# Delta-rule blocks in a fixed order, with the decay prepared a head ahead

## The chip, the cores and the metric

One core of a Trainium2 chip runs one program. The metric is the device time of one execution in microseconds; the figure for a kernel is the median of several. The core has TensorE (PE, with its weight loader PEld), VectorE (DVE), ScalarE (ACT), GpSimd (POOL), and SyncE (SP), which here issues the DMAs.

## The reference

A hybrid decoder layer on x of 2048 x 1024, all float32: a norm, one input projection of 9224 columns, two token mixers side by side, and an output projection. The part that matters here is the first mixer, gated DeltaNet with 4 heads of 128 channels, in chunks of 64 tokens:

```python
qkv = silu(causal_depthwise_conv(dn_qkv, conv_w))      # 4 taps
q = l2_normalize(q) * 128 ** -0.5;  k = l2_normalize(k)
gc = cumsum(g)                                         # per chunk, per head
decay = exp(where(causal, gc[i] - gc[j], -inf))
lower = where(strict, (beta * k) @ k.T * decay, 0)
a_intra = where(causal, q @ k.T * decay, 0)
# then (I + lower)^-1, u, w, and a scan over the chunks
```

The second mixer is a dilated sliding-window attention; its part of the kernel is not changed.

## The kernel before

The program runs in stages: attention with its projections; three projection units for gates (`z_block`), beside which the last attention tiles drain; the delta-rule stage; the remaining gate units, beside which VectorE inverts the chunk matrices and the scan runs; and the output.

In the delta-rule stage `cunits` goes through twelve units, for each head h one of keys, one of queries, one of values (`k_block`, `q_block`, `v_block`). A unit has 4 blocks of 512 tokens. A block is 24 matmuls of 128x512 into a PSUM tile `mm` (three buffers): float32 is split in a high and a low part, three products for each of 8 slices. After every second slice `self.hook()` runs, so a hook is six wide matmuls and a block four hooks. `self.at(d, f)` runs `f` d hooks later. It is the way in which small TensorE work of a block (transposes, key-key and query-key products) is put between the wide matmuls of later blocks. `fn(n, pr)` is the block's function, called when its 24 matmuls are issued.

`conv` copies the block to `xr` (ScalarE), multiplies by the last tap into `acc` (ScalarE), adds three taps (VectorE, L629), takes a tanh (ScalarE) and multiplies (VectorE, L632), all at once in the program. `k_block` then loads the cumulated decay of the block, broadcast over 128 partitions, into `gcb` (512 KB, one buffer), adds the causal mask (VectorE, L650), takes four differences (L654) and four exponentials into `E` (ScalarE, L656). At hooks 8 and 9 it transposes the keys in pairs (L663) and ScalarE empties the two PSUM tiles `tp`, with a sum of squares (L667) and a scaling (L668). `q_block` splits keys and queries into a high part `kqh` (ScalarE) and a low part `kql` (L699 on GpSimd for keys, L701 on VectorE for queries), whole blocks with one buffer; at hooks 8 and 9 it transposes queries (L709) and multiplies (L710 to L712) into `sc`, and VectorE multiplies by `E` into `la` (L715), which five DMAs store. `v_block` transposes and scales.

What sets the order: in this stage nothing is fixed by hand. The framework's scheduler orders each engine's instructions by its own estimate of times and by buffers. In the attention stage `pinned` fixes the order of PE, ACT, DVE and POOL as written; SP's, after the first loads, is the scheduler's.

Of the kernel before, what the change touches and what calls it, by code (L numbers as in the profile page):

```python
# [6 lines left out]
F32 = mybir.dt.float32  # L7
# [5 lines left out]
P = 128  # L13
# [3 lines left out]
NB = 4  # L17
# [23 lines left out]
class Net:  # L41
# [574 lines left out]
    def conv(self, n, ct, pr, dst):  # L616
        nc, dp = self.nc, self.dp
        xr = dp.tile([P, 515], F32, name="xr", bufs=2)
        if n == 0:
            nc.gpsimd.memset(xr[:, 0:3], 0.0)  # L620
        else:
            nc.vector.tensor_copy(xr[:, 0:3], self.xr[:, 512:515])
        self.xr = xr
        nc.scalar.activation(xr[:, 3:515], pr, AF.Copy)
        acc = dp.tile([P, 512], F32, name="acc", bufs=2)
        w = self.cw[:, ct, :]
        nc.scalar.activation(acc, pr, AF.Identity, scale=w[:, 3:4])  # L627
        for j in (2, 1, 0):
            nc.vector.scalar_tensor_tensor(out=acc, in0=xr[:, j:j + 512], scalar=w[:, j:j + 1], in1=acc,  # L629
                                           op0=ALU.mult, op1=ALU.add)  # L630
        nc.scalar.activation(dst, acc, AF.Tanh, scale=0.5)
        nc.vector.scalar_tensor_tensor(out=dst, in0=dst, scalar=1.0, in1=acc, op0=ALU.add, op1=ALU.mult)  # L632
# [4 lines left out]

    def k_block(self, h, n, pr):
        nc, dp = self.nc, self.dp
        if n == 0:  # L640
            self.kT = dp.tile([P, T], F32, name="kT", bufs=1)
            self.E = dp.tile([P, 16, P], F32, name="E", bufs=1)
        kT, E = self.kT[:, n * 512:(n + 1) * 512], self.E
        self.conv(n, 4 + h, pr, kT)
        self.recput(n, h, R_KT, P, kT.rearrange("p (a c) -> p a c", c=P))
        gcb = dp.tile([P, 2, 4, P], F32, name="gcb", bufs=1)
        nc.sync.dma_start(gcb.rearrange("p a b c -> p a (b c)"),
                          dr(self.gcscr, h * T + n * 512, [[0, P], [H * T, 2], [1, 512]]))
        En = E[:, n * 4:n * 4 + 4, :]
        nc.vector.tensor_tensor(out=gcb[:, 1], in0=gcb[:, 1], in1=self.cmask.unsqueeze(1).to_broadcast([P, 4, P]),  # L650
                                op=ALU.add)
        for t in range(4):
            c = h * 16 + n * 4 + t
            nc.vector.scalar_tensor_tensor(out=gcb[:, 0, t], in0=gcb[:, 0, t], scalar=self.ngc[:, c:c + 1],  # L654
                                           in1=gcb[:, 1, t], op0=ALU.add, op1=ALU.add)
            nc.scalar.activation(En[:, t, :], gcb[:, 0, t], AF.Exp, bias=self.nlc[:, c:c + 1])  # L656
        ss = dp.tile([P, 12], F32, name="ss", bufs=2)
        kd = dp.tile([P, 4, P], F32, name="st4", bufs=2)

        def pe(t0):  # L660
            pt = self.ps.tile([P, 512], F32, name="tp", bufs=2)
            for t in (t0, t0 + 1):
                nc.tensor.transpose(pt[:, (t - t0) * P:(t - t0 + 1) * P], kT[:, t * P:(t + 1) * P], self.ident)  # L663
            for t in (t0, t0 + 1):
                c = h * 16 + n * 4 + t
                a = pt[:, (t - t0) * P:(t - t0 + 1) * P]
                nc.scalar.activation(kd[:, t, :], a, AF.Square, accum_out=ss[:, t:t + 1])  # L667
                nc.scalar.activation(kd[:, t, :], a, AF.Identity, scale=self.ek[:, c:c + 1])  # L668
            if t0 == 2:
                fin()  # L670

        def fin():
            cs = slice(h * 16 + n * 4, h * 16 + n * 4 + 4)
            self.recput(n, h, R_KD, P, kd)
            G = nc.gpsimd
            G.tensor_scalar(out=ss[:, 0:4], in0=ss[:, 0:4], scalar1=4 * EPS, scalar2=None, op0=ALU.add)
            G.tensor_tensor(out=ss[:, 4:8], in0=ss[:, 0:4], in1=self.mhalf[:, 0:4], op=ALU.pow)
            G.tensor_tensor(out=ss[:, 8:12], in0=ss[:, 4:8], in1=self.beta[:, cs], op=ALU.mult)
            G.tensor_scalar(out=self.vss[:, cs], in0=ss[:, 8:12], scalar1=0.5, scalar2=None, op0=ALU.mult)
            G.tensor_tensor(out=ss[:, 8:12], in0=ss[:, 8:12], in1=ss[:, 4:8], op=ALU.mult)  # L680
            G.tensor_scalar(out=self.nbr[:, cs], in0=ss[:, 8:12], scalar1=-1.0, scalar2=None, op0=ALU.mult)
            G.tensor_tensor(out=self.ksn[:, cs], in0=self.nbr[:, cs], in1=self.egc[:, cs], op=ALU.mult)
        self.at(8, lambda: pe(0))
        self.at(9, lambda: pe(2))

    def q_block(self, h, n, pr):
        nc, dp = self.nc, self.dp
        qT = dp.tile([P, 512], F32, name="qT", bufs=2)
        self.conv(n, h, pr, qT)
        self.recput(n, h, R_QT, P, qT.rearrange("p (a c) -> p a c", c=P))  # L690
        kT, E = self.kT, self.E
        ss = dp.tile([P, 12], F32, name="ss", bufs=2)
        sq = dp.tile([P, P], F32, name="sq", bufs=1)
        kqh = dp.tile([P, 4, 2, P], F32R, name="kqh", bufs=1)
        kql = dp.tile([P, 4, 2, P], F32R, name="kql", bufs=1)
        la = dp.tile([P, 4, 2, P], F32, name="la", bufs=1)
        kv, qv = (a.rearrange("p (a c) -> p a c", c=P) for a in (kT[:, n * 512:(n + 1) * 512], qT))
        nc.scalar.activation(kqh[:, :, 0, :], kv, AF.Copy)
        nc.gpsimd.tensor_tensor(out=kql[:, :, 0, :], in0=kv, in1=kqh[:, :, 0, :].bitcast(F32), op=ALU.subtract)  # L699
        nc.scalar.activation(kqh[:, :, 1, :], qv, AF.Copy)  # L700
        nc.vector.tensor_tensor(out=kql[:, :, 1, :], in0=qv, in1=kqh[:, :, 1, :].bitcast(F32), op=ALU.subtract)  # L701

        def pe(t0):
            pt = self.ps.tile([P, 512], F32, name="tp", bufs=2)
            pk = self.ps.tile([P, 512], F32, name="sc", bufs=2)
            for t in (t0, t0 + 1):
                b = pk[:, (t - t0) * 256:(t - t0) * 256 + 256]
                rh, rl = (a[:, t].rearrange("p a c -> p (a c)") for a in (kqh, kql))
                nc.tensor.transpose(pt[:, (t - t0) * P:(t - t0 + 1) * P], qT[:, t * P:(t + 1) * P], self.ident)  # L709
                nc.tensor.matmul(b, kqh[:, t, 0, :], rh, start=True, stop=False)  # L710
                nc.tensor.matmul(b, kqh[:, t, 0, :], rl, start=False, stop=False)
                nc.tensor.matmul(b, kql[:, t, 0, :], rh, start=False, stop=True)  # L712
            for t in (t0, t0 + 1):
                nc.scalar.activation(sq, pt[:, (t - t0) * P:(t - t0 + 1) * P], AF.Square, accum_out=ss[:, t:t + 1])
            nc.vector.tensor_tensor(out=la[:, t0:t0 + 2], in0=pk.rearrange("p (a b c) -> p a b c", b=2, c=P),  # L715
                                    in1=E[:, n * 4 + t0:n * 4 + t0 + 2, :].unsqueeze(2).to_broadcast([P, 2, 2, P]),
                                    op=ALU.mult)
            if t0 == 2:
                cs = slice(h * 16 + n * 4, h * 16 + n * 4 + 4)
# [6 lines left out]
                G = nc.gpsimd  # L726
                G.tensor_scalar(out=ss[:, 0:4], in0=ss[:, 0:4], scalar1=4 * EPS, scalar2=None, op0=ALU.add)
                G.tensor_tensor(out=ss[:, 4:8], in0=ss[:, 0:4], in1=self.mhalf[:, 0:4], op=ALU.pow)
                G.tensor_scalar(out=self.cq[:, cs], in0=ss[:, 4:8], scalar1=SCALE, scalar2=None, op0=ALU.mult)
        self.at(8, lambda: pe(0))  # L730
        self.at(9, lambda: pe(2))

    def v_block(self, h, n, pr):
        nc, dp = self.nc, self.dp
        vT = dp.tile([P, 512], F32, name="qT", bufs=2)
        self.conv(n, 8 + h, pr, vT)
# [10 lines left out]
        self.at(8, pe)  # L747
# [284 lines left out]
    def run(self):  # L1032
# [27 lines left out]

        def open_dn():
# [3 lines left out]
            self.dp = pool(dst, "dp", "right")  # L1065

        def start_inverse():
            self.nb_out()
            dst.close()
# [103 lines left out]
```

## Time and profile before

| | |
|---|---|
| device time, median of 3 | 2399.8 us (2398.44 to 2401.62) |
| profiled execution | 2395.87 us, span 2394.1 us |
| granted TensorE clock, mean | 0.995 |
| TensorE busy | 2350.5 us, 98% |
| delta-rule stage | about 1118 to 1430 us of the span |

Times in the views count from the start of the span. An idle time stands before the instruction that ended it, with what released it. Busy TensorE time is the union of its matmuls, whose ends are modelled: wide ones show some 0.39 us each but start closer together.

### The profile page before, as it was taken

The page shows a single profiled execution, that of the slowest core. Times are in us where ns is not written, and L with a number is a line of the kernel's source. Part 1 is how long each engine was busy: PE and PEld are TensorE (multiplying, and loading weights), DVE is VectorE, ACT ScalarE, POOL GpSimd, SP SyncE. Part 2 cuts the span into 40 slices and gives each one's busy share as a digit, 9 for nine tenths or more (in the row PEclk, how much of TensorE's full clock was granted, in tenths as well). Part 3 has the DMA queues.
Part 4 walks back from the last instruction along what each step waited for, and adds up shares of the span by engine and source line. Part 5 has one row for each costly group of instructions (what it writes and reads, how often), then busy time and mean ns, then how long its engine had stood idle before and what let it go on. Part 6 is the DMA issues. An engine that isn't in the chain of part 4 may idle for free.

```text
span 2394.1 us, 40632 instructions
## 1 busy us (share of the span) xinstructions
PE 2350.5 (98%) x13640; PEld 2136.8 (89%) x13640; DVE 1169.7 (49%) x2819; ACT 856.6 (36%) x3021; POOL 824.0 (34%) x1803
## 2 busy tenths in 40 slices
PE   8999999999999999999999999999999999999999
PEld 7899999999999999988777878888888878889988
DVE  5543344334434434344666666999344433454431
ACT  6433333444434444334665662111233313111110
POOL 6633333333333334301442451101233212433441
PEclk9999999999999999999999999999999999999999
DMA  8443344333333335233454443222567645555442
GB/s 283 156 115 111 107 122 120 104 101 108 109 97 111 111 91 128 85 94 103 126 128 117 117 106 118 68 75 75 191 203 207 184 150 158 155 175 161 147 141 75
DMA packets 378808, 307.30 MB, mean 128 GB/s; under 512 B 61352, under 2 KB 345320, under 8 KB 378216
## 3 DMA queue, kind: packets, MB, share of 16 engines
q1 hardware_dynamic: 378312, 304.64, 43.5%
q8 instruction: 108, 1.77, 0.3%
q14 instruction: 100, 0.82, 0.1%
q10 hardware_dynamic: 288, 0.07, 0.0%
HBM read 187.92 MB, written 116.69 MB: 127 GB/s over the span
## 4 chain that ended last, share of the span: by engine, by line
PE 86%; DMA 4%; DVE 3%; POOL 3%; ACT 2%; issue 2%; SPq 0%; ACTq 0%; DVEq 0%; POOLq 0%
PE mm L238 10%; PE mm L240 10%; PE mm L239 10%; PE mm L524 9%; PE mm L526 9%; PE mm L525 9%; PE mm L1014 2%; PE mm L1016 2%; PE mm L1015 2%; PE mm L997 2%; PE mm L999 2%; PE mm L998 2%; DMA gcb<-gcscr 2%; PE po L333 2%; PE tp L290 2%
## 5 line engine op out<-in xcount | busy, mean ns | idle before, releaser
L238 PE MATMUL mm<-wh,hh 128*128 128x384 f32 (+1 forms) x1536 | 554.4, 361 | 6.1 <-ACT hh L131 2.7
L240 PE MATMUL mm<-wh,hl 128*128 128x384 f32 (+1 forms) x1536 | 519.3, 338 | 2.7 <-DVE hl L135 2.7
L239 PE MATMUL mm<-wl,hh 128*128 128x384 f32 (+1 forms) x1536 | 517.8, 337 | 0.7 <-DVE wl L79 0.6
L524 PE MATMUL mm<-hh,wh 128*128 128x512 f32 x1152 | 464.8, 403 | 0.0
L526 PE MATMUL mm<-hh,wl 128*128 128x512 f32 x1152 | 454.5, 395 | 0.0
L525 PE MATMUL mm<-hl,wh 128*128 128x512 f32 x1152 | 453.1, 393 | 0.0
L238 PEld LDWEIGHTS mm<-wh,hh 128*128 128x128 f32 x1536 | 289.6, 189 | 10.5 <-ACT wh L78 4.3
L240 PEld LDWEIGHTS mm<-wh,hl 128*128 128x128 f32 x1536 | 288.9, 188 | 4.1 <-DVE hl L135 4.1
L239 PEld LDWEIGHTS mm<-wl,hh 128*128 128x128 f32 x1536 | 290.5, 189 | 1.7 <-DVE wl L79 1.1
L526 PEld LDWEIGHTS mm<-hh,wl 128*128 128x128 f32 x1152 | 217.3, 189 | 47.3
L524 PEld LDWEIGHTS mm<-hh,wh 128*128 128x128 f32 x1152 | 217.6, 189 | 43.0
L525 PEld LDWEIGHTS mm<-hl,wh 128*128 128x128 f32 x1152 | 217.8, 189 | 41.2
L263 DVE SCALAR_TENSOR_TENSOR rec<-mm,st,wqk 128x128 f32<-128x128 f32 x384 | 116.7, 346 | 264.4 <-POOL st L255 239.4
L79 POOL TENSOR_TENSOR wl<-raw,wh 128x512 fp32r<-128x512 f32 (+1 forms) x73 | 104.2, 1439 | 409.4 <-ACT wh L78 409.2
L317 ACT ACTIVATE p<-sc,ol 128x128 f32<-128x128 f32 (+1 forms) x192 | 82.0, 427 | 315.8 <-DVE ol L315 273.3
L253 POOL TENSOR_SCALAR st<-st 128x2 f32<-128x2 f32 x192 | 37.7, 196 | 400.9 <-ACT rec L249 399.5
L249 ACT ACTIVATE rec<-mm 128x128 f32<-128x128 f32 x384 | 102.4, 272 | 185.3 <-PE mm L240 171.3
L997 PE MATMUL mm<-oh,hh 128*128 128x256 f32 x512 | 143.8, 281 | 3.1 <-DVE gt L1001 2.9
L999 PE MATMUL mm<-oh,hl 128*128 128x256 f32 x512 | 142.9, 279 | 0.0
L998 PE MATMUL mm<-ol,hh 128*128 128x256 f32 x512 | 142.9, 279 | 0.0
L629 DVE SCALAR_TENSOR_TENSOR acc<-xr,cw,acc 128x512 f32<-128x512 f32 x144 | 121.7, 845 | 41.9 <-ACT acc L627 37.7
L255 POOL TENSOR_TENSOR st<-st,mhalf 128x2 f32<-128x2 f32 x192 | 134.7, 702 | 16.0
(243 smaller groups left out, 4283.8 us busy)
## 6 DMA issues: line engine op xcount, KB each, us to landing
rscr<-rec SPq DMA_DIRECT2D x192, 192.0 KB, 1.9
raw<-in_w_in_dram SPq DMA_DIRECT2D x138, 256.0 KB, 3.0
qk<-rscr SPq DMA_DIRECT2D x192, 128.0 KB, 2.2
gscr<-gt SPq DMA_DIRECT2D x64, 256.0 KB, 2.4
gt<-gscr SPq DMA_DIRECT2D x64, 256.0 KB, 3.4
oscr<-ol SPq DMA_DIRECT2D x192, 65.0 KB, 2.0
oc<-oscr SPq DMA_DIRECT2D x16, 780.0 KB, 5.2
v<-rscr SPq DMA_DIRECT2D x192, 64.0 KB, 2.0
```

What stands on the lines that cost most here:

```text
L238: nc.tensor.matmul(pr[:, :w], a, wh[:, k, :w], start=(k == 0), stop=False)
L239: nc.tensor.matmul(pr[:, :w], a, wl[:, k, :w], start=False, stop=False)
L240: nc.tensor.matmul(pr[:, :w], b, wh[:, k, :w], start=False, stop=(k == KT - 1))
L255: nc.gpsimd.tensor_tensor(out=st[:, 2:4], in0=st[:, 0:2], in1=self.mhalf[:, 0:2], op=ALU.pow)
L263: nc.vector.scalar_tensor_tensor(out=qk[:, j, :], in0=pr[:, j * P:(j + 1) * P], scalar=st[:, 2 + j:3 + j], in1=s["w"][2][:, j, :], op0=ALU ...
L524: nc.tensor.matmul(pr, wh[:, k, :], a, start=(k == 0), stop=False)
L525: nc.tensor.matmul(pr, wh[:, k, :], b, start=False, stop=False)
L526: nc.tensor.matmul(pr, wl[:, k, :], a, start=False, stop=(k == KT - 1))
L629: nc.vector.scalar_tensor_tensor(out=acc, in0=xr[:, j:j + 512], scalar=w[:, j:j + 1], in1=acc, op0=ALU.mult, op1=ALU.add)
L997: nc.tensor.matmul(o, self.wbh[:, k, ms], oh[:, k, :], start=(k == b * 4), stop=False)
L998: nc.tensor.matmul(o, self.wbh[:, k, ms], ol[:, k, :], start=False, stop=False)
L999: nc.tensor.matmul(o, self.wbl[:, k, ms], oh[:, k, :], start=False, stop=(k == b * 4 + 3))
```

## The change

- The order of PE, ACT, DVE and POOL is fixed as written (`pinned(False)`: SP's is not) from `open_dn`, ahead of the first key unit, to `start_inverse`.
- The decay is a chain of its own, `e_chain`: load at its start, mask 4 hooks later (now on GpSimd), differences after 5 (VectorE, straight into `E`), exponentials after 7, in place. Head 0's blocks start 7 hooks apart at the stage's beginning; head h + 1's start with the first value block of head h, 5 hooks apart. `E` has four buffers of one block; `gcb` still has one.
- In `conv` tanh and the last multiply (`gate`) come 4 hooks later, right ahead of the next block's convolution. For keys and queries the first tap moves to VectorE; the clearing of `xr` too.
- Key transposes at hooks 7 and 9, their sums at 11; values at 7.
- `kqh` and `kql` are made in pairs of 128 tokens, two buffers, both low parts on GpSimd, at hooks 6 and 7; query products at 9 and 10, with both transposes ahead of the six products; the sums at 12.

```diff
-    def conv(self, n, ct, pr, dst):
+    def conv(self, n, ct, pr, dst, then):
...
-            nc.gpsimd.memset(xr[:, 0:3], 0.0)
+            nc.vector.memset(xr[:, 0:3], 0.0)
...
-        nc.scalar.activation(acc, pr, AF.Identity, scale=w[:, 3:4])
+        if ct < 8:
+            nc.vector.tensor_scalar(out=acc, in0=pr, scalar1=w[:, 3:4], scalar2=None, op0=ALU.mult)
+        else:
+            nc.scalar.activation(acc, pr, AF.Identity, scale=w[:, 3:4])
...
-        nc.scalar.activation(dst, acc, AF.Tanh, scale=0.5)
-        nc.vector.scalar_tensor_tensor(out=dst, in0=dst, scalar=1.0, in1=acc, op0=ALU.add, op1=ALU.mult)
+        def gate():
+            nc.scalar.activation(dst, acc, AF.Tanh, scale=0.5)
+            nc.vector.scalar_tensor_tensor(out=dst, in0=dst, scalar=1.0, in1=acc, op0=ALU.add, op1=ALU.mult)
+            then()
+        self.at(4, gate)
...
+    def e_chain(self, h, period, n=0):
+        if h == H:
+            return
+        nc, dp = self.nc, self.dp
+        gcb = dp.tile([P, 2, 4, P], F32, name="gcb", bufs=1)
+        nc.sync.dma_start(gcb.rearrange("p a b c -> p a (b c)"),
+                          dr(self.gcscr, h * T + n * 512, [[0, P], [H * T, 2], [1, 512]]))
+        def mask():
+            nc.gpsimd.tensor_tensor(out=gcb[:, 1], in0=gcb[:, 1],
+                                    in1=self.cmask.unsqueeze(1).to_broadcast([P, 4, P]), op=ALU.add)
+        def diff():
+            E = self.E[h, n] = dp.tile([P, 4, P], F32, name="E", bufs=4)
+            for t in range(4):
+                c = h * 16 + n * 4 + t
+                nc.vector.scalar_tensor_tensor(out=E[:, t, :], in0=gcb[:, 0, t], scalar=self.ngc[:, c:c + 1],
+                                               in1=gcb[:, 1, t], op0=ALU.add, op1=ALU.add)
+        def expo():
+            E = self.E[h, n]
+            for t in range(4):
+                c = h * 16 + n * 4 + t
+                nc.scalar.activation(E[:, t, :], E[:, t, :], AF.Exp, bias=self.nlc[:, c:c + 1])
+        self.at(4, mask)
+        self.at(5, diff)
+        self.at(7, expo)
+        if n + 1 < NB:
+            self.at(period, lambda: self.e_chain(h, period, n + 1))
...
-        self.at(8, lambda: pe(0))
+        self.at(7, lambda: pe(0))
         self.at(9, lambda: pe(2))
+        self.at(11, fin)
...
-        nc.scalar.activation(kqh[:, :, 0, :], kv, AF.Copy)
-        nc.gpsimd.tensor_tensor(out=kql[:, :, 0, :], in0=kv, in1=kqh[:, :, 0, :].bitcast(F32), op=ALU.subtract)
-        nc.scalar.activation(kqh[:, :, 1, :], qv, AF.Copy)
-        nc.vector.tensor_tensor(out=kql[:, :, 1, :], in0=qv, in1=kqh[:, :, 1, :].bitcast(F32), op=ALU.subtract)
+        def prep(t0):
+            kqh = dp.tile([P, 2, 2, P], F32R, name="kqh", bufs=2)
+            kql = dp.tile([P, 2, 2, P], F32R, name="kql", bufs=2)
+            kq[t0] = kqh, kql
+            for j, src in enumerate((kv, qv)):
+                nc.scalar.activation(kqh[:, :, j, :], src[:, t0:t0 + 2, :], AF.Copy)
+                nc.gpsimd.tensor_tensor(out=kql[:, :, j, :], in0=src[:, t0:t0 + 2, :], in1=kqh[:, :, j, :].bitcast(F32),
+                                        op=ALU.subtract)
...
-        self.at(8, lambda: pe(0))
-        self.at(9, lambda: pe(2))
+        self.at(6, lambda: prep(0))
+        self.at(7, lambda: prep(2))
+        self.at(9, lambda: pe(0))
+        self.at(10, lambda: pe(2))
+        self.at(12, fin)
...
-        self.conv(n, 8 + h, pr, vT)
+        self.conv(n, 8 + h, pr, vT, lambda: None)
+        if n == 0:
+            self.e_chain(h + 1, 5)
...
-        self.at(8, pe)
+        self.at(7, pe)
...
+            pin.enter_context(pinned(False))
+            self.E = {}
+            self.e_chain(0, 7)
...
+            pin.close()
```

How the instructions stand, at three places. First VectorE where head 0's values end and head 1's keys begin (`qT` is also the tile of the values). Before, from the last value block's taps on:

```order
L629 SCALAR_TENSOR_TENSOR acc<-xr,cw,acc 128x512 x3
L632 SCALAR_TENSOR_TENSOR qT<-qT,acc 128x512
L622 COPY xr<-xr 128x3
L650 TENSOR_TENSOR gcb<-gcb,cmask 128x512
L654 SCALAR_TENSOR_TENSOR gcb<-gcb,ngc 128x128 x3
L629 SCALAR_TENSOR_TENSOR acc<-xr,cw,acc 128x512
L654 SCALAR_TENSOR_TENSOR gcb<-gcb,ngc 128x128
L629 SCALAR_TENSOR_TENSOR acc<-xr,cw,acc 128x512 x2
L632 SCALAR_TENSOR_TENSOR kT<-kT,acc 128x512
```

and after, at the same place:

```order
L632 SCALAR_TENSOR_TENSOR acc<-xr,cw,acc 128x512 x3
L662 SCALAR_TENSOR_TENSOR E<-gcb,ngc 128x128 x4
L637 SCALAR_TENSOR_TENSOR qT<-qT,acc 128x512
L620 MEMSET xr 128x3
L628 TENSOR_SCALAR acc<-mm,cw 128x512
L632 SCALAR_TENSOR_TENSOR acc<-xr,cw,acc 128x512 x3
L662 SCALAR_TENSOR_TENSOR E<-gcb,ngc 128x128 x4
L637 SCALAR_TENSOR_TENSOR kT<-kT,acc 128x512
```

The four differences now stand together between a convolution and that block's gate, and the last set of head 1 stands ahead of its first `kT`.

Second, TensorE at a pair of query products. Before:

```order
L709 MATMUL tp<-ident,qT 128x128
L710 MATMUL sc<-kqh 128x256
L711 MATMUL sc<-kql,kqh 128x256
L712 MATMUL sc<-kqh,kql 128x256
L709 MATMUL tp<-ident,qT 128x128
```

and after:

```order
L737 MATMUL tp<-ident,qT 128x128 x2
L741 MATMUL sc<-kqh 128x256
L742 MATMUL sc<-kql,kqh 128x256
L743 MATMUL sc<-kqh,kql 128x256
L741 MATMUL sc<-kqh 128x256
```

Both transposes moved ahead of the six products; the first product that needs `kql` is now the fourth instruction, not the third.

Third, SP's queue after, at head 1's value unit (`st` are records of value blocks, `raw` weights, `gcb` the decay of head 1's second block and then of the third, fourth and head 2's first):

```order
L651 DMA gcb<-gcscr 128x2x512
L642 DMA rec<-la 128x4x128
L642 DMA rec<-la 64x4x64
L754 DMA lscr<-la 64x4x64 x2
L642 DMA rec<-st_14954 128x4x128
L503 DMA raw<-in_w_in_dram 128x4x128
L651 DMA gcb<-gcscr 128x2x512
L642 DMA rec<-st_15045 128x4x128
L642 DMA rec<-st_15138 128x4x128
L651 DMA gcb<-gcscr 128x2x512 x2
L642 DMA rec<-st_15197 128x4x128
```

Each decay load stands behind the records and weights that are due ahead of it, in the order of their due times.

More of the change, by code (lines that the diff above doesn't have):

```diff
@@ L641, in k_block @@
             self.kT = dp.tile([P, T], F32, name="kT", bufs=1)
[L642 to L657, printed above, removed]
+        kT = self.kT[:, n * 512:(n + 1) * 512]
+        self.conv(n, 4 + h, pr, kT, lambda: self.recput(n, h, R_KT, P, kT.rearrange("p (a c) -> p a c", c=P)))
+        ss = dp.tile([P, 12], F32, name="ss", bufs=3)
         kd = dp.tile([P, 4, P], F32, name="st4", bufs=2)
@@ L669, in pe @@
             if t0 == 2:
-                fin()
+                self.recput(n, h, R_KD, P, kd)
         def fin():
             cs = slice(h * 16 + n * 4, h * 16 + n * 4 + 4)
-            self.recput(n, h, R_KD, P, kd)
             G = nc.gpsimd
@@ L1059, in run @@
         xo = {}
+        pin = ExitStack()
         def open_dn():
```

36 lines of the change are left out of this document (19 added, 17 removed).

## Prediction

> **What bounds the kernel now.** The page comes first: TensorE is busy for nearly the whole span, so a change elsewhere can save at most what TensorE loses.
>
> ```profile
> span 2394.1 us, 40632 instructions
> PE 2350.5 (98%) x13640; PEld 2136.8 (89%) x13640; DVE 1169.7 (49%) x2819; ACT 856.6 (36%) x3021; POOL 824.0 (34%) x1803
> ```
>
> The windows then say in which stage it is lost (columns: length, PE, weight loads, VectorE, ScalarE, GpSimd, granted clock, DMA share, GB/s).
>
> ```profile
> 0.00:100.00 100.00, 84.89 (x454) 79.46 (x454) 61.37 (x186) 61.25 (x176) 70.48 (x146) 0.97 0.71 235
> 1000.00:1450.00 450.00, 436.62 (x2202) 360.93 (x2201) 271.66 (x536) 250.60 (x780) 155.56 (x245) 1.00 0.43 112
> 1450.00:1900.00 450.00, 448.99 (x2427) 378.67 (x2426) 297.22 (x517) 113.51 (x341) 96.67 (x198) 1.00 0.45 135
> 1118.00:1430.00 312.00, 299.38 (x1463) 245.18 (x1462) 212.67 (x345) 197.53 (x623) 135.25 (x206) 0.99 0.47 119
> ```
>
> The last window is the delta-rule stage, the only one that the change touches. TensorE idles 312.00 - 299.38 = 12.6 us there, and nobody else is full (VectorE 68%, ScalarE 63%, GpSimd 43%). So it waits for things that come late, not for a full engine. The waits of TensorE and of its weight loader in that window name them (total, times, longest):
>
> ```profile
> PE tp L663 <- ACT st L668: 8.4, 6, 2.9
> PE sc L711 <- POOL kql L699: 2.7, 3, 2.0
> PE sc L711 <- DVE kql L701: 1.4, 4, 0.3
> PEld tp L663 <- ACT st L668: 11.9, 9, 3.4
> PEld sc L711 <- POOL kql L699: 3.8, 5, 2.2
> PEld sc L711 <- issue: 2.0, 4, 0.5
> ```
>
> Key transposes (L663) wait for ScalarE to empty the PSUM tile two transposes earlier; query products (L711) wait for the low halves `kql`. Why is ScalarE late? The chain of waits in the first key blocks:
>
> ```profile
> 1126.96 4.56 DMA gcb<-gcscr
> 1131.55 0.69 DVE gcb L650
> 1132.32 0.32 DVE gcb L654
> 1132.66 1.29 ACT E L656 x4
> 1133.97 5.05 DMA gcb<-gcscr
> ```
>
> One buffer `gcb` goes round: load, mask, differences, exponentials, next load, 7.0 us a turn here. Exponentials and differences stand in the queues between evacuations, so ScalarE and VectorE wait for a DMA with TensorE's work behind it.
>
> **The worth of the waits.** The PE rows give 8.4 + 2.7 + 1.4 = 12.5 us, in 13 waits. That is a lower bound, since a matmul's end is modelled later than the next could start:
>
> ```profile
> 1289.28 0.40 PE L525 MATMUL mm<-hl,wh 128*128 128x512 f32 x1
> 1289.51 0.39 PE L526 MATMUL mm<-hh,wl 128*128 128x512 f32 x1
> 1300.27 0.40 PE L526 MATMUL mm<-hh,wl 128*128 128x512 f32 x1
> 1303.61 0.44 PE L663 MATMUL tp<-ident,kT 128*128 128x128 f32 x2 [2.95 <-ACT st L668]
> 1300.00:1310.00 10.00, 7.05 (x26) 5.33 (x26) 5.74 (x12) 6.80 (x25) 4.39 (x9) 0.83 0.40 114
> ```
>
> Wide matmuls start 0.23 us apart. From 1300.27 to 1303.61 are 3.34 us, so 3.11 are lost where the row says 2.95: 0.16 more a wait, 2.1 for thirteen. The upper bound is the weight loader's 11.9 + 3.8 + 2.0 = 17.7. I take 12.5 + 2.1 = 14.6. After that longest wait the window shows a granted clock of 0.83 for 10 us: 1.7 us more. Together 16.3 us, between 12.5 and 19.4.
>
> The Trainium skill ("TensorE: Matmul & The Clock Gate", section "What's actually happening") halves the clock after an idle window of about 3.4 us. The drop here followed 2.95 us of idle, so the measured row decides; by the page shorter waits cost only themselves and the 1.7 would not return with new waits of 3 us.
>
> **What the change makes of each.**
>
> *Key transposes, 8.4 us idle.* They move from hooks 8 and 9 after their block to 7 and 9. A hook is six wide matmuls, 6 x 0.23 = 1.4 us, so ScalarE has 2.8 us instead of 1.4 to empty a tile. The four exponentials no longer stand in front of it, and the tanh, now a block behind, finds its convolution done. I count these waits as gone. What is late next is `kT` itself: it is due 3 hooks (4.1 us) after its gate is queued, and needs one tanh and one VectorE operation of 0.69. That leaves over 2 us, except where decay differences stand ahead of the gate (below).
>
> *Query products, 4.1 us idle.* `kql` is made at hooks 6 and 7 for products at 9 and 10. Two half subtractions on GpSimd (half of 1435 ns each, next fence) and two ScalarE copies take some 2 us of 4.1. Gone. Transposes and products are the same number, in another order; the trace has no row for two transposes in front, so 0, bounded by 0.1 us a group of 32 either way (3 us, inside the range).
>
> *Work moved between engines* (rows of the stage):
>
> ```profile
> L627 ACT ACTIVATE acc<-mm,cw 128x512 f32<-128x512 f32 x46 | 31.9, 693 | 0.0
> L79 POOL TENSOR_TENSOR wl<-raw,wh 128x512 fp32r<-128x512 f32 x22 | 30.4, 1384 | 27.0 <-ACT wh L78 26.9
> L699 POOL TENSOR_TENSOR kql<-kT,kqh 128x512 fp32r<-128x512 f32 x16 | 23.0, 1435 | 52.3 <-ACT kqh L698 35.3 <-DMA rec<-kT 16.4
> L715 DVE TENSOR_TENSOR la<-sc,E 128x512 f32<-128x512 f32 x31 | 20.8, 682 | 5.6 <-DMA lscr<-la 5.5
> L701 DVE TENSOR_TENSOR kql<-qT,kqh 128x512 fp32r<-128x512 f32 x16 | 15.6, 974 | 2.1 <-ACT kqh L700 2.1
> L654 DVE SCALAR_TENSOR_TENSOR gcb<-gcb,ngc 128x128 f32<-128x128 f32 x64 | 19.6, 347 | 0.4
> L650 DVE TENSOR_TENSOR gcb<-gcb,cmask 128x512 f32<-128x512 f32 x16 | 13.3, 830 | 25.4 <-DMA gcb<-gcscr 25.3
> L632 DVE SCALAR_TENSOR_TENSOR kT<-kT,acc 128x512 f32<-128x512 f32 x16 | 11.1, 691 | 8.5 <-ACT kT L631 8.5
> L629 DVE SCALAR_TENSOR_TENSOR acc<-xr,cw,acc x138: 735/752/1890, 1120.6 to 1429.7; 128x512 f32<-128x512 f32 x138
> DMA to landing us min/median/max: 4.6/5.1/6.7
> ```
>
> ScalarE gives 32 x 0.69 = 22 us of tap multiplies to VectorE (32 x 0.68, by L715, which also reads PSUM); VectorE gives 13.3 of masks and 15.6 of `kql` to GpSimd (16 x 1.38 and 16 x 1.44). All stay under 75% of 312 us. Cost 0, hidden under TensorE.
>
> *The decay load, a head ahead.* Here I see the price. Head 0 starts a turn every 7 hooks (9.6 us). Heads 1 to 3 ask for one every 5, from the first value block of the head before, with one `gcb` buffer still. A turn is now load 5.1 + mask on GpSimd 1.38 + four differences 4 x 0.35 = 7.9 us, against 5 x 1.4 = 6.9 us. On VectorE each set of differences stands between a convolution and the next block's gate, and the last gate is the next head's first `kT`. TensorE's time from the end of the second value block to those key transposes is 19 hooks, 26.2 us, and what lies between:
>
> ```profile
> 1288.60 0.60 PE L742 MATMUL tp<-ident,qT 128*128 128x128 f32 x4
> 1250.08 0.27 PE L709 MATMUL tp<-ident,qT 128*128 128x128 f32 x1
> 1251.01 0.39 PE L524 MATMUL mm<-hh,wh 128*128 128x512 f32 x1
> ```
>
> Four value transposes take 1289.28 - 1288.60 - 0.23 = 0.45 us (four sets), a product group 0.93 (two): 29.9 us in all. The other side: two evacuations (at most 0.69 each), three taps of 0.75 and the first differences 1.4 make 5.0; three turns 23.7; the gate 0.69: 29.4. VectorE is also held up by GpSimd now and then: L629's longest is 1890 ns against a median of 752. One or two such hits put TensorE's wait at about 1.2 us a head, between 0 (load 4.6, no hit) and 3: 3.6 us for three heads, 0 to 9. Behind the waiting differences stand the gate and the next convolution; only the transposes wait for these, three PSUM buffers hide the rest.
>
> *Start of the stage.* The order of the last attention tiles moves a little; nothing there waits long, so 0, give or take 0.5:
>
> ```profile
> PEld po L332 <- ACT pT L326: 0.8, 3, 0.3
> ```
>
> **The sum.** -16.3 + 3.6 = -12.7 us. The profiled execution took 2395.87 (span 2394.1 and 1.8 around it), 3.9 under the median 2399.8; I set the saving against the median: 2387.1 us.
>
> **Rivals.**
>
> *The decay turn costs more* (each load about 1 us late, 3 us or so a head): -16.3 + 9 to 12 leaves 2392 to 2396. For: the one buffer. Against: the first load of a head is fetched early and the second finds slack. 0.18.
>
> *VectorE becomes the bound of query blocks.* It has 3 x 0.75 + 0.69 + 0.68 + 2 x 0.68 = 5.0 us a block; if every GpSimd subtraction (4 x 0.72) blocked it, 7.9 us against TensorE's 24 x 0.23 + 2 x 0.93 = 7.4. Sixteen blocks x 0.5 = 8 us: 2395, no change to speak of. For: 1890 against 752. Against: most of the 5.0 falls before the copies that start the subtractions, and the L715 products read PSUM. 0.08. The Trainium skill ("SBUF — State Buffer", section "Who interferes with whom") says it as a rule: VectorE with two SBUF inputs and a GpSimd operation that reads SBUF share one locked port pair and the later one blocks; the 1890 agrees.
>
> *The fixed order opens other waits*, ScalarE or VectorE standing at an input that a scheduler would have passed by: 5 to 10 us of the 16 come back, about 2395. Every edge that I followed has 1 to 2 us of slack. 0.07.
>
> *Slower:* the three loads of a turn-around land at the longest value, 6.7: 3 x 1.6 = 4.8 more, 6.0 us of wait a head, and after such a wait the clock drop of 1.7: 3 x 7.7 = 23 us against 16.3, so 2407. It decides from a mean landing of about 5.9. The median 5.1 speaks against it, the second load of a head, beside weights and records, for it. 0.07. By the clock rule above the same follows, since 6 us exceed its window.
>
> **How the numbers follow.** The forecast case (2380 to 2391) has 0.60. Two tenths of a per cent, 4.8 us, is what a measurement tells from no change. Faster: 0.60, most of the first rival and a little of the third, 0.77. Same: the rest of these and the second, 0.15. Slower 0.08. The range goes from 2380 (upper bound of the waits, nothing paid back) to 2395, which takes in the first rival; the others, 0.2, lie at or above its end.
>
> **What would show it.** Right: in the stage's window TensorE idles 3 to 5 us, L663's and L711's successors wait for nothing but at heads' starts, where the first key transposes of heads 1 to 3 wait for VectorE's `kT`, about 1 us each, and the clock stays 1.00. The `E` differences wait for GpSimd's mask, and that for the load. Wrong: waits over 3 us at the heads' starts with a dropped clock; or query products that still wait for `kql`; or TensorE idle unchanged with other names.

## The result, and the profile after

The changed kernel takes 2384.95 us (median of 4, 2383.94 to 2386.20) beside 2399.12 for the kernel before (median of 4, 2394.47 to 2401.62). The ratio is 0.995, with a 95% interval of 0.9935 to 0.9964: 14.2 us faster, and 10.9 in a later group of runs (E12: 2386.53 against 2397.38, ratio 0.9951, 0.9937 to 0.9964). The forecast was 2387.1, 12.7 us faster.

The head of the page, after. TensorE does the same 13640 matmuls in a span that is 11.7 us shorter; VectorE and GpSimd are busier, by 22 and 62 us, at 50% and 37% of the span.

```profile
span 2382.4 us, 40700 instructions
PE 2343.1 (98%) x13640; PEld 2133.7 (90%) x13640; DVE 1191.4 (50%) x2831; ACT 847.5 (36%) x3021; POOL 886.0 (37%) x1855
```

The windows of the changed kernel (length, then busy time of TensorE, its weight loads, VectorE, ScalarE and GpSimd, granted clock, DMA share, GB/s). The second row lies behind the delta stage: 448.99 us busy, as before. In the stage TensorE idles 312.00 - 305.46 = 6.5 us, where it was 12.6.

```profile
1000.00:1450.00 450.00, 442.68 (x2253) 368.12 (x2252) 297.62 (x553) 243.39 (x786) 215.04 (x298) 1.00 0.42 113
1450.00:1900.00 450.00, 448.99 (x2426) 378.70 (x2425) 298.91 (x526) 111.83 (x337) 98.05 (x198) 1.00 0.46 140
1118.00:1430.00 312.00, 305.46 (x1513) 252.34 (x1513) 240.69 (x363) 192.87 (x636) 198.29 (x264) 1.00 0.47 123
```

The waits of TensorE in the stage, after (total, times, longest). The waits for ScalarE's evacuations are gone and those for `kql` nearly so. What is left has a new name: key transposes wait for `kT` itself.

```profile
PE tp L688 <- DVE kT L637: 5.4, 4, 2.1
PE sc L742 <- POOL kql L728: 0.8, 3, 0.3
PE sc L741 <- ACT qT L636: 0.3, 1, 0.3
```

A fixed window cuts off different work in a faster kernel, so the stage is better measured between two instructions: from the first key transposes of head 0 to the last value transposes of head 3. The TensorE timeline before has

```profile
1130.08 0.38 PE L663 MATMUL tp<-ident,kT 128*128 128x128 f32 x2
...
1451.52 0.60 PE L742 MATMUL tp<-ident,qT 128*128 128x128 f32 x4
```

and after, with the first key transposes of each head:

```profile
1129.62 0.38 PE L688 MATMUL tp<-ident,kT 128*128 128x128 f32 x2
...
1211.21 0.44 PE L688 MATMUL tp<-ident,kT 128*128 128x128 f32 x2 [2.08 <-DVE kT L637]
...
1290.15 0.44 PE L688 MATMUL tp<-ident,kT 128*128 128x128 f32 x2 [1.00 <-DVE kT L637]
...
1368.91 0.44 PE L688 MATMUL tp<-ident,kT 128*128 128x128 f32 x2 [0.95 <-DVE kT L637]
...
1440.60 0.60 PE L780 MATMUL tp<-ident,qT 128*128 128x128 f32 x4
```

The stage fell from 321.44 to 310.98 us, 10.5 of the 11.7. The same reading for every kernel of this study (heads 0 to 2 from first key transposes to the next head's, head 3 to its last value transposes):

| kernel | head 0 | head 1 | head 2 | head 3 | stage | time, us |
|---|---|---|---|---|---|---|
| before | 83.01 | 81.46 | 83.05 | 73.92 | 321.44 | 2399.12 |
| changed | 81.59 | 78.94 | 78.76 | 71.69 | 310.98 | 2384.95 |
| E1 decay chain alone | 89.91 | 81.60 | 81.65 | 72.47 | 325.63 | 2400.26 |
| E2 no fixed order | 92.71 | 86.44 | 85.69 | 75.26 | 340.10 | 2413.25 |
| E3 turn of 7 hooks | 79.34 | 77.70 | 77.69 | 71.74 | 306.47 | 2381.09 |
| E4 decay in its own head | 82.20 | 81.81 | 81.85 | 75.88 | 321.74 | 2395.83 |
| E5 gate at once | 91.77 | 90.96 | 91.90 | 86.20 | 360.83 | 2435.02 |
| E6 splits one hook ahead | 88.05 | 84.97 | 86.28 | 75.86 | 335.16 | 2409.70 |
| E7 mask on VectorE | 80.39 | 77.91 | 77.74 | 71.70 | 307.74 | 2383.60 |
| E8 E3, head 0 later | 85.09 | 77.70 | 77.58 | 71.61 | 311.98 | 2387.25 |
| E9 E3, first exponentials later | 82.12 | 77.70 | 77.57 | 71.62 | 309.01 | 2381.56 |
| E10 E9, head 0 masks on VectorE | 79.08 | 77.57 | 77.56 | 71.64 | 305.85 | 2380.45 |
| E11 half the load | 77.99 | 77.70 | 77.57 | 71.62 | 304.88 | 2381.99 |
| E12 changed again | 83.08 | 79.31 | 79.34 | 71.81 | 313.54 | 2386.53 |

A head nearly without waits takes 77.56 us and the last one 71.61 (the least values of the table), so 304.3 in all. Against this floor the kernel before lost 17.1 us and the changed one 6.7. The last row is the changed kernel a second time: its stage is 2.6 us longer, 1.4 of it by a drop of the clock in head 0 (last section). So differences of this size between two rows, each of one execution, are not resolved by the rows alone. Where these 6.7 come from is seen in the chain of waits at the start of head 1:

```profile
1193.85 5.46 DMA gcb<-gcscr
...
1199.47 1.29 POOL gcb L655
...
1202.00 4.93 DMA gcb<-gcscr
...
1207.10 1.29 POOL gcb L655
1208.39 0.02 issue
1208.41 2.14 DVE E L662 x4
1210.56 0.61 DVE kT L637
1211.17 0.04 issue
1211.21 0.44 PE tp L688 x2
```

Load, mask, differences, next load: from the mask at 1199.47 to that at 1207.10 are 7.6 us (7.3 at the same place in the next two heads), against the 6.9 at which turns are asked for. The last set of differences stands on VectorE ahead of the gate that makes `kT`, and TensorE waits behind that.

### The profile page after: what moved, and what is told of

It reads as the page before. It is cut to its first block, busy times and chain, and to the rows that moved or that the text cites. A ratio compares the mean times of both kernels' runs of the same rounds, so it can differ in the third digit from the quotient of the medians.

```text
span 2382.4 us, 40700 instructions
## 1 busy us (share of the span) xinstructions
PE 2343.1 (98%) x13640; PEld 2133.7 (90%) x13640; DVE 1191.4 (50%) x2831; ACT 847.5 (36%) x3021; POOL 886.0 (37%) x1855
## 4 chain that ended last, share of the span: by engine, by line
PE 85%; POOL 4%; DMA 4%; DVE 4%; ACT 2%; issue 2%; SPq 0%; POOLq 0%; ACTq 0%; DVEq 0%
PE mm L240 10%; PE mm L238 10%; PE mm L239 10%; PE mm L524 9%; PE mm L526 9%; PE mm L525 9%; PE mm L1054 2%; PE mm L1052 2%; PE mm L1053 2%; PE mm L1035 2%; PE mm L1037 2%; PE mm L1036 2%; PE po L333 2%; PE tp L290 2%; DMA gcb<-gcscr 1%
```

## The experiments

All were run in five rounds beside the kernel before on the same chip. E1 to E4, E5 to E8 and E9 to E12 are three groups, in which the kernel before took 2397.12, 2399.23 and 2397.38 us; times of different groups can be compared no closer than these agree. Two ask what earned the gain (E1, E2), four take one part of the change back or move it (E4 to E7), five work on the 6.7 us that are left (E3, E8 to E11), and E12 repeats the changed kernel.

**E1, the decay chain alone** on the kernel before (`e_chain` and its two calls; the code in `k_block` that it replaces is gone).

```diff
+        if n == 0:                       # v_block
+            self.e_chain(h + 1, 5)
+            self.e_chain(0, 7)           # open_dn
```

> The kernel before with one part of the change: the decay loads, masks (GpSimd), differences and exponentials run as a chain of their own, for head h+1 from the value blocks of head h. Order of the scheduler, tanh, convolution, key and query splits as before. Theory A (the exponentials and differences that wait for the load stand ahead of the evacuations of the key transposes): the 8.4 us of waits of key transposes for ScalarE fall under 2 us, the clock drop goes, some 3 us come back where differences stand ahead of the first key gates, the query products still wait some 4 us for kql: about 2391 to 2394, ratio 0.997. Theory B (the order written by hand earned it): the key transposes wait as long as before, 2397 or more, ratio 0.999 to 1.000.

Measured: 2400.26 us, ratio 1.0015 (1.0006 to 1.0024). It is 3 us slower than the kernel before in its group: no gain by itself. Theory B's "2397 or more" takes the time in, but its waits did not come. TensorE's waits from 1080 to 1450:

```profile
PE sc L729 <- POOL kql L717: 8.0, 6, 2.2
PE tp L681 <- ACT st L686: 3.7, 3, 2.1
PE sc L729 <- DVE kql L719: 3.5, 3, 1.6
```

Key transposes lost more than half of their waits (8.4 to 3.7), though not as far as theory A had it. The query products took them over: 11.5 us for `kql`, before 4.1. GpSimd has the mask in addition now; at the first such wait its timeline shows a mask from 1159.68 and then 8.9 us of the norms' small operations, all ahead of the subtraction, which starts at 1169.89. So 8.0 of the 11.5 moved to the queue that was given the work; the 3.5 for VectorE's half are not explained by that, and no run separates them. The heads differ, too. In heads 1 to 3, whose decay is a head ahead, no key transpose waits any more (6.6 us before) and the three heads are 2.7 us shorter. Head 0, whose decay cannot be ahead, is 6.9 us longer, with its waits for evacuations up from 1.9 to 3.7 us and two drops of the clock.

**E2, the changed kernel without the fixed order.**

```diff
-            pin.enter_context(pinned(False))
```

> The changed kernel without the fixed order in the delta stage: the scheduler orders the engines, everything else stays. Theory A (decay ahead and splits ahead earned it): within 2 us of the changed kernel, 2383 to 2387, TensorE idle 6 to 8 us in the stage. Theory B (the fixed order earned it): TensorE's idle time in the stage returns to 10 us or more, 2389 to 2396.

Measured: 2413.25 us, ratio 1.0067 (1.0054 to 1.0079), 16 us slower than the kernel before in its group and 28 slower than with the fixed order. Theory B by more than it asked. TensorE waits for the same two things as in the kernel before, for `kql` three times as long:

```profile
PE sc L742 <- POOL kql L728: 13.7, 10, 2.4
PE tp L688 <- ACT st L693: 7.8, 5, 3.9
```

ScalarE's timeline ahead of the longest shows what the scheduler does with the exponentials: it puts one between the two halves of an evacuation (L692 and L693), where it waits 2.54 us for the differences.

```profile
1150.11 0.26 ACT L692 ACTIVATE st<-tp 128x128 f32<-128x128 f32 x1
1150.27 0.19 ACT L692 ACTIVATION_READ_ACCUMULATOR st<-tp 128x1 f32 x1
1153.00 0.40 ACT L669 ACTIVATE E<-E,nlc 128x128 f32<-128x128 f32 x1 [2.54 <-DVE E L662]
1153.31 0.35 ACT L693 ACTIVATE st<-tp,ek 128x128 f32<-128x128 f32 x1
```

So the decay chain, the late gate and the early splits together gain only with an order that keeps them at their hooks. The fixed order alone on the kernel before was not tried: with its single buffers for the pairs, the order as written has the next block's split ahead of the products that still read the last one.

**E3, a turn of 7 hooks for heads 1 to 3.**

```diff
-            self.e_chain(h + 1, 5)
+            self.e_chain(h + 1, 7)
```

> The changed kernel with a decay turn every 7 hooks (9.6 us) for heads 1 to 3 instead of every 5 (6.9). Theory A (a turn of 7.9 us with one buffer does not fit 6.9 us, and the late differences stand ahead of the next head's first key gate): the waits of the first key transposes of heads 1 to 3 for kT, 4.5 us in the records of the changed kernel, fall under 1 us; head 0's 1.5 us stay; about 2380.5, ratio to before 0.9925. Rival C (GpSimd's mask and the low weight halves behind it hold VectorE up, wherever the differences stand): the waits stay or move to other key gates, 2384 to 2386.

Measured: 2381.09 us, ratio 0.993 (0.9918 to 0.9943). Theory A. Heads 1 and 2 are at the floor (77.70, 77.69), and one wait for `kT` is left, head 0's. The edit does two things at once: turns no longer press on each other, and the last set of differences falls behind the first key gate (it starts at 1216.49, the first key transposes at 1208.88). E7 and E11, where it still stands ahead, show that a shorter turn is enough.

```profile
PE tp L688 <- DVE kT L637: 1.5, 1, 1.5
```

**E4, the decay chain in its own head** (7 hooks a turn, so that it differs from E3 in the place alone).

```diff
+            self.e_chain(h, 7)           # k_block, n == 0
-            self.e_chain(h + 1, 7)       # v_block
-            self.e_chain(0, 7)           # open_dn
```

> The changed kernel with the decay chain of every head begun in that head's own first key block, a turn every 7 hooks, and nothing a head ahead. Theory A: now four sets of differences and exponentials a head fall among key and query blocks as head 0's do in the changed kernel (1.5 us of wait there), in part ahead of key gates: 1 to 3 us a head more than with the same turn a head ahead, 2383 to 2393 in all. Rival D (a fixed place in the queues and GpSimd's mask are what counts, a head ahead adds nothing): as the run with a turn of 7 hooks within 1.5 us.

Measured: 2395.83 us, ratio 0.9994 (0.9985 to 1.0003): 14.7 us above E3, past theory A's end. Heads 1 to 3 pay 4.1 to 4.2 us each against E3, and most of it is not at the gates that theory A named:

```profile
PE sc L743 <- POOL kql L729: 11.0, 4, 2.8
PE tp L689 <- DVE kT L637: 4.5, 4, 1.4
```

The first is one wait a head, in its first query block. ScalarE and GpSimd there, in head 0 (one fence each):

```profile
1152.65 1.27 ACT L669 ACTIVATE E<-E,nlc 128x128 f32<-128x128 f32 x4
1153.83 0.40 ACT L728 ACTIVATE kqh<-kT 128x256 fp32r<-128x256 f32 x1
```

```profile
1154.31 0.74 POOL L729 TENSOR_TENSOR kql<-kT,kqh 128x256 fp32r<-128x256 f32 x1 [1.20 <-ACT kqh L728]
...
1156.17 0.22 POOL L701 TENSOR_SCALAR ss<-ss 128x4 f32<-128x4 f32 x1
...
1160.73 0.72 POOL L729 TENSOR_TENSOR kql<-kT,kqh 128x256 fp32r<-128x256 f32 x1
```

Four exponentials ahead of the `kqh` copies hold these up, GpSimd stands 1.20 us for the copy, and the key block's norm chain (4.6 us of small operations) is ahead of the second pair. Begun a head ahead, all four sets are over by the last key blocks, ahead of the first splits.

**E5, tanh and gate at once.**

```diff
-        self.at(4, gate)
+        gate()
```

> The changed kernel with tanh and gate queued right behind their own convolution, not four hooks later. Theory A (a tanh that waits for its taps holds ScalarE, with evacuations behind it): the tanh waits 2 to 3 us a block for VectorE, and key transposes or query products wait again, 2 to 6 us more than the changed kernel: 2387 to 2391. Rival E (ScalarE has slack there, and a gate ahead of the late differences frees the first key transposes): the 5.4 us of waits for kT go and nothing comes, 2379 to 2381.

Measured: 2435.02 us, ratio 1.0148 (1.0135 to 1.0162), 50 us slower than the changed kernel: theory A's mechanism at eight times the end of its range. Of ScalarE's waits in the stage, the tanh's for VectorE's convolution are the two largest:

```profile
ACT kT L636 <- DVE acc L632: 62.1, 16, 5.0
ACT qT L636 <- DVE acc L632: 35.7, 12, 4.3
```

They take 3.9 and 3.0 us in the mean, over two hooks of 1.4 us, and ScalarE's evacuations and `kqh` copies stand behind it: TensorE waits 25.3 us for evacuations and 11.2 for `kqh`. Half of rival E came: no wait for `kT` is left, which it had forecast of a gate that stands ahead of the late differences. In a fixed order, an operation placed right behind its producer holds everything that was written later.

**E6, pairs one hook ahead of their products.**

```diff
-        self.at(6, lambda: prep(0))
-        self.at(7, lambda: prep(2))
+        self.at(8, lambda: prep(0))
+        self.at(9, lambda: prep(2))
```

> The changed kernel with the key and query pairs made one hook before their products instead of three. A hook is 1.4 us, two copies on ScalarE (0.4 each) and two subtractions on GpSimd (0.74 each) take about 2.3. Theory A (the distance is what removed the waits for kql): about 1 us of wait in each of 16 query blocks, 2395 to 2402. Rival F (the halves alone, which let the first products start on half the work, did it): under 3 us of waits for kql, 2385 to 2388.

Measured: 2409.70 us, ratio 1.004 (1.0027 to 1.0054). Theory A: sixteen blocks, sixteen waits of 1.17 us in the mean. The time is 8 us past its range. At the first of them (2.0 us) GpSimd runs a mask and a norm chain, from 1155.34 to 1160.84, ahead of the subtraction whose copies were done at 1156.5: the hooks' distance and the queue's other work add up.

```profile
PE sc L742 <- POOL kql L728: 18.7, 16, 2.2
```

**E7, the mask on VectorE.**

```diff
-            nc.gpsimd.tensor_tensor(out=gcb[:, 1], in0=gcb[:, 1],
+            nc.vector.tensor_tensor(out=gcb[:, 1], in0=gcb[:, 1],
```

> The changed kernel with the decay mask on VectorE instead of GpSimd, all else alike. Rival C (GpSimd's mask and what runs behind it on GpSimd lengthen VectorE's differences): the differences take 1.1 us a set everywhere, the waits of the first key transposes for kT halve, 2381 to 2383. Theory A (the turn of 7.9 us against 6.9 is the cause): a turn is now 5.1 + 0.83 + 1.4 = 7.3, waits fall by a third at most, and VectorE stands before the load with convolutions behind it: 2383 to 2388.

Measured: 2383.60 us, ratio 0.9935 (0.9923 to 0.9948), not to be told from the changed kernel. Inside it two things cancel. Heads 1 and 2 are near the floor (77.91, 77.74): the mask takes 0.69 us there, and the last two sets of differences ahead of a head start 6.5 to 6.7 us apart (7.3 to 7.6 in the changed kernel), which fits 6.9. Rival C expected shorter differences everywhere. They did not come: the last set of every head still takes 2.07 us (at 1211.50, 1289.41 and 1367.14, beside a weight half on GpSimd), and the waits at the heads' starts went all the same. So it is the turn, as theory A has it, though its sum, with 0.83 and 1.4 for the mask and the differences, had left two thirds of the waits. But VectorE now stands before the first load with head 0's first convolution behind the mask, and the first key transposes come at 1133.84 instead of 1129.62, after a wait of 2.44 us.

**E8, head 0's differences and exponentials four hooks later**, on E3.

```diff
-        self.at(5, diff)
-        self.at(7, expo)
+        late = 4 if h == 0 else 0
+        self.at(5 + late, diff)
+        self.at(7 + late, expo)
```

> The run with a turn of 7 hooks, and for head 0 alone the differences and exponentials four hooks later. Theory A (what is left there is head 0's exponentials, which wait for the load with the tanh of its first key gate behind them): the remaining 1.5 us wait for kT goes, 2379.5 against 2381.1, no wait over 0.5 us in the stage. Rival G (head 0 is late because its attention tiles end late, and the later differences fall ahead of the next gate): the wait stays or moves, 2381 to 2383.

Measured: 2387.25 us, ratio 0.9948 (0.9936 to 0.9961), 6 us above E3 (5.5 in the stage); both theories missed. The wait for `kT` is gone, and one of 5.62 us for `kql` has come. GpSimd's timeline:

```profile
1146.99 1.40 POOL L655 TENSOR_TENSOR gcb<-gcb,cmask 128x512 f32<-128x512 f32 x1 [5.32 <-DMA gcb<-gcscr]
...
1157.60 1.72 POOL L655 TENSOR_TENSOR gcb<-gcb,cmask 128x512 f32<-128x512 f32 x1
1159.28 1.17 POOL L729 TENSOR_TENSOR kql<-kT,kqh 128x256 fp32r<-128x256 f32 x1
```

Later differences free the buffer later, the next load lands later, and its mask holds GpSimd for 5.32 us with two norm chains and the first `kql` behind. The masks were left where they were; that was the slip.

**E9, only head 0's first exponentials later**, on E3.

```diff
-        self.at(7, expo)
+        self.at(11 if h == n == 0 else 7, expo)
```

> The run with a turn of 7 hooks, and of head 0 only the first block's exponentials four hooks later, behind its first tanh and not ahead of it. Theory A (these exponentials delay the first key gate by 1.3 us, and this passes down to the third key block): the remaining wait of 1.5 us for kT shrinks by 0.4 to 1.5, 2379.6 to 2380.7 against 2381.1. Rival G (the third gate hangs on the second turn's load and mask, not on the first gate): the wait stays 1.5, 2381.

Measured: 2381.56 us, ratio 0.9935 (0.9923 to 0.9947), no change from E3 in the times, and the wait for `kT` has grown to 2.6 us: rival G. (The stage of the profiled execution is 2.5 us longer than E3's, 1.5 of it by a drop of the clock behind that wait.) The tanh comes earlier, and so does the weight split behind it; GpSimd's half of that now runs beside the first differences. VectorE in E3 (first row of its fence) and in E9 (second):

```profile
1126.31 1.14 DVE L662 SCALAR_TENSOR_TENSOR E<-gcb,ngc 128x128 f32<-128x128 f32 x4 [2.44 <-POOL gcb L655]
```

```profile
1126.57 2.18 DVE L662 SCALAR_TENSOR_TENSOR E<-gcb,ngc 128x128 f32<-128x128 f32 x4 [2.67 <-POOL gcb L655]
```

E9's GpSimd timeline at that place:

```profile
1126.49 1.32 POOL L79 TENSOR_TENSOR wl<-raw,wh 128x512 fp32r<-128x512 f32 x1
```

The first gate had waited 1.08 us for its tanh in E3. That microsecond was lost again in the differences.

**E10, E9 with head 0's second to fourth mask on VectorE.**

```diff
-            nc.gpsimd.tensor_tensor(out=gcb[:, 1], in0=gcb[:, 1],
+            (nc.vector if h == 0 < n else nc.gpsimd).tensor_tensor(out=gcb[:, 1], in0=gcb[:, 1],
```

> As the run before, and the masks of head 0's second to fourth block on VectorE instead of GpSimd. Theory A with rival G's second half (the mask on GpSimd and the low weight halves that run behind it make the second set of differences 2.2 us instead of 1.1): the set takes 1.1 to 1.5 us, the mask 0.83 instead of 1.3, and the last wait for kT is under 0.3 us: 2379 to 2380. If VectorE, standing before the load, delays convolutions instead: 2381 to 2383.

Measured: 2380.45 us, ratio 0.9928 (0.9916 to 0.9941). The second set of differences and its mask, on VectorE:

```profile
1134.51 0.69 DVE L655 TENSOR_TENSOR gcb<-gcb,cmask 128x512 f32<-128x512 f32 x1 [1.56 <-DMA gcb<-gcscr]
1135.24 1.14 DVE L662 SCALAR_TENSOR_TENSOR E<-gcb,ngc 128x128 f32<-128x128 f32 x4
```

1.14 us where E9 had 2.13, and the wait for `kT` is 0.35; one for `qT` has grown from 0.3 to 1.1. Against E3 the gain is not resolved by the times; against the changed kernel of the same group (E12) it is 6.1 us, with no overlap of the single runs (2377.66 to 2382.24 against 2384.51 to 2389.85). It has the lowest median of all, and E3, a change of one number, gives most of it.

**E11, half the load**: the changed kernel without the low word of the cumulated decay.

```diff
-                          dr(self.gcscr, h * T + n * 512, [[0, P], [H * T, 2], [1, 512]]))
+                          dr(self.gcscr, h * T + n * 512, [[0, P], [1, 512]]))
-                                               in1=gcb[:, 1, t], op0=ALU.add, op1=ALU.add)
+                                               in1=self.cmask, op0=ALU.add, op1=ALU.add)
-        self.at(4, mask)
```

> The changed kernel, a turn every 5 hooks, without the low word of the cumulated decay: half the load and no mask operation (the mask is added in the difference itself), so the decay is less exact. Theory A (load and mask make the turn 7.9 us against 6.9): the turn is 3.5 to 4.6 of load and 1.1 of differences, under 6.9, and the waits for kT of heads 1 to 3 (4.5 us) go, head 0's shrinks: 2379 to 2380.5. Rival C (VectorE's differences are late for want of GpSimd's port, whenever the load lands): at least half of the 4.5 us stays, 2382 or more.

Measured: 2381.99 us, ratio 0.9936 (0.9924 to 0.9948). Theory A: the load lands in 3.4 us (median; 4.9 with both words), no wait for `kT` is left though turns are asked for every 5 hooks, and the stage has the least loss of all, 304.88. As the mask operation is gone too, this run doesn't say how much either of them gave. The median is 1.5 us above the expected range.

**E12, the changed kernel again.** No edit.

> The changed kernel once more, beside the runs of this group on the same chip. Every theory: 2384 to 2386, four waits of key transposes for kT, 5.4 us together.

Measured: 2386.53 us, ratio 0.9951 (0.9937 to 0.9964); four waits for `kT`, 6.3 us together instead of 5.4 (1.93 in head 0, then 1.40, 1.53 and 1.42), and the granted clock fell after the first. The median is half a microsecond past the expected.

## Why the prediction was right, and where it was not

*The waits go: right.* 16.3 us were forecast (14.6 of waits, 1.7 of clock). The loss against the floor was 17.1, and of the old waits 0.8 us is left, for `kql`; one of 0.3, for `qT`, is new. The lower bound, the 12.5 of the rows, was 4.6 too low, and the correction of 0.16 a wait and the clock term cover most of that. The term of 0 for the other order of the products held: a group takes 0.93 us, as before (from 1182.83 to 1183.76, for instance).

*The decay turn pays back at the heads' starts: right in place and size.* Forecast 1.2 us a head; measured 2.08, 1.00 and 0.95 in the rows, with 0.16 each 4.5 us in place of 3.6 (4.8 in E12). With head 0's 1.5 (below) and 0.7 of other small losses these are the 6.7. E3 (turns asked for less often), E7 (shorter mask) and E11 (shorter load, no mask) each remove it. The terms: load 5.46 and 4.93, with 0.36 for its issue (taken 5.1), mask 1.29 (1.38), four differences 1.14 when free (1.4). The turn was 7.6, 7.3 and 7.3 and not 7.9. The single hit from GpSimd in the working was there in each of the three heads: 2.14 to 2.17 instead of 1.14 us, in head 1 with a weight half starting on GpSimd at 1208.34, right behind the mask.

*The start of the stage costs nothing, give or take 0.5: wrong.* Head 0 waited 1.37 us at its third key block. The step that failed is the one that gave every gate "over 2 us" of slack "except where decay differences stand ahead of the gate" and then looked for this only in heads 1 to 3. Head 0's turns run beside its own key blocks, so its differences stand ahead of key gates. Ahead of the one that was late, VectorE's copy, three taps and differences took 1.28, 3.24 and 2.18 us, each with a 128x512 operation on GpSimd beside it; free of that they take 0.16, 2.33 and 1.14. Its exponentials stand ahead of the first tanh, which I took for the cause after the result; E9 moved them away and the wait stayed. With that edit in place, E10 took the mask and with it the stretched differences (2.13 us to 1.14) away, and the wait went.

*Work moved costs nothing: right in sum, but not because engines have room.* VectorE came to 240.69 of 312 us, 77%, past the 75% named. By the forecast's own moves it would have come to 212.67 + 22 - 13.3 - 15.6 = 206. Half of the 35 us above that is one line, the copy of three elements at the start of a convolution, before and after:

```profile
L622 DVE COPY xr<-xr 128x3 f32<-128x3 f32 x35 | 5.8, 166 | 12.4 <-ACT xr L624 12.3
```

```profile
L622 DVE COPY xr<-xr 128x3 f32<-128x3 f32 x35 | 23.5, 671 | 0.0
```

The copies, like other operations of VectorE, got longer where GpSimd's weight halves and `kql` subtractions now run beside them (last section), and this item of the forecast had no term for it. E1 shows the `kql` queue with a mask and norms ahead of it costing 8.0 us. What hid it is where each operation stands.

*The rivals.* Loads did not land late (4.6 to 5.2 us, median 4.9). Query blocks did not become VectorE's: TensorE's waits for `kql` and `qT` came to 1.1 us in all. The slower case needed landings of 6.7. The fixed order, which stood there only as a risk of 0.07, turned out to be the part without which there is no gain (E2). The forecast summed the parts one by one; the decay chain alone is worth nothing (E1), and everything but the order is a loss of 16 us (E2).

*The sum.* -12.7 us forecast; -10.5 in the stage and -11.7 in the span of the profiled executions; -14.2 and -10.9 in the medians of two groups. The two groups differ by 3.3 us, so an agreement of the time closer than that is luck. In the stage the sum was 2.2 too large: 16.3 - 3.6 against 17.1 - 6.7, since the 6.7 hold head 0's 1.5, 0.9 more at the heads' starts and 0.7 of small losses. And the sign that the clock stays at 1.00 held in the one profiled execution and not in the other (E12).

## What to carry to other kernels

Where an engine's queue is fixed, ask of each instruction what it waits for and what is written behind it: an operation that waits for a DMA or for another engine's chain belongs at the hook where its input has landed, and late for one queue can be early for the next (E8, E9). Compare the time of one turn of a buffer, with every operation on it, with the time between requests, since 0.4 to 0.7 us too much here stood ahead of a gate in every head, and asking less often (E3) or a shorter turn (E7) cured it. Parts of such a change aren't additive: test it by taking parts away from the whole, not only by adding them to the old kernel.

## What the runs showed of the hardware that was not expected

The clock. In E4 the same wait of 2.75 us comes once in each head. Windows of 5 us from each resumption, the first head's and the second's:

```profile
1162.09:1167.09 5.00, 4.90 (x17) 4.18 (x18) 3.12 (x5) 2.14 (x6) 5.00 (x7) 0.66 0.51 124
1245.32:1250.32 5.00, 4.90 (x24) 4.09 (x25) 3.10 (x5) 2.11 (x6) 5.00 (x7) 1.00 0.53 129
```

The granted clock fell to 0.66 in the first and stayed at 1.00 in the other three. In E2 it fell after 2.01 us of idle time and not after 2.42; in the changed kernel it did not after 2.08. When the same kernel ran again (E12), it fell after 1.93:

```profile
1139.17 0.44 PE L688 MATMUL tp<-ident,kT 128*128 128x128 f32 x2 [1.93 <-DVE kT L637]
1139.17:1144.17 5.00, 5.00 (x17) 3.97 (x18) 4.20 (x8) 2.47 (x8) 1.70 (x6) 0.66 0.86 237
```

So no length of idle time between 2 and 3 us decides it here. The Trainium skill ("TensorE: Matmul & The Clock Gate", "What's actually happening") has a window of about 3.4 us that runs free of the kernel: such a window would make the phase decide, as seen here, though these drops came after less idle time than a whole window. The 1.7 us of the forecast is thus an expense that comes in some heads and not in others, and in one execution of a kernel and not in another. A wide matmul takes 0.43 us from start to start after a drop and 0.23 otherwise (E9, 1139.4 to 1142.0).

VectorE beside GpSimd. Four differences took 1.14 us alone and 2.13 to 2.19 when a `wl` subtraction of 1.3 us was running beside them. A copy of three elements (L622) took 1.29 us instead of 0.16 in E3, when it started 0.04 us behind such a subtraction; in the changed kernel this happened to 12 of the 35 copies of the window, and 8 more took 0.70 us beside a `kql` subtraction. The Trainium skill's rule of one locked port pair ("SBUF — State Buffer", "Who interferes with whom") fits: the later one waits for the whole of the other.
